# Feeding the output projection from psum in one inference step: last head pair, chunk rows, value tiles and conv state rearranged

## The chip, the cores and the metric

The kernel runs on one core of one Trainium2 chip. The core has five engines with an instruction queue each: TensorE (PE; its weight loads are listed apart as PEld), VectorE (DVE), ScalarE (ACT), GpSimd (POOL) and SyncE (SP, which only issues transfers). Each engine takes its instructions in the order in which they were compiled and waits at an instruction until the semaphores that it names are there. The metric is the device time in microseconds (us) of one execution, the median of several runs.

## The reference, cut to what matters

One layer of a decoder: a combined input projection, two kinds of token mixing side by side (attention heads and pooling), one output projection for both, and a gated feed-forward with a causal convolution. It runs once over a prompt of 2048 tokens behind 16 meta tokens, and once over 8 samples of one token with a paged cache of 4096 keys and values each.

```python
h = rmsnorm(xp, norm_mix_g)
q, k, v, u = project_mix(h, w_in)
o_attn = stick_breaking(q, k, v, q_pos, k_pos, sb_bias)       # 8 heads of 64
o_pool = multiscale_pool(u, 0, T, pool_w, pool_scale)
xp = xp + jnp.concatenate([o_attn, o_pool], axis=-1) @ w_out  # 1024 x 1024
h2 = rmsnorm(xp, norm_ffn_g)
f, conv_prompt = conv_ffn(h2, zero_prefix, w_up, conv_w, conv_b, w_down)   # d_ff 2816
y_prompt = rmsnorm(xp + f, norm_final_g)[:, N_META:]
...
k_past = cache_k[page_table].reshape(DB, PAST_LEN, H_A, DH)   # samples
v_past = cache_v[page_table].reshape(DB, PAST_LEN, H_A, DH)
f, conv_sample = conv_ffn(h2, state_conv, w_up, conv_w, conv_b, w_down)
```

## The kernel before, in words

Large products are taken three times: each operand is split into a rounded high part and the low rest (`split`, L162: ACT casts, L163, DVE subtracts, L164), and `mm3` (L166) adds high by high, high by low and low by high (L169 to L171). The text calls the products by the psum tile that they fill: pso (output projection), psu (up-projection), psd (down-projection).

**Attention.** Four head pairs are worked through, the last with hp = 3, in blocks of 128 queries (bi); a block runs over chunks of 512 keys from the last to the first. `top` marks a block's first chunk and `low` its last. `weigh` (L531) transposes the weights (tt) and multiplies them with the values into the psum tile po. At `low` a copy of po (ot, on DVE) is written to the DRAM buffer cat_s, which holds the concatenated mixer output in eight chunks of 128 rows: four of the head pairs, four of the pooling. `finished` collects the blocks of the last pair.

**Output projection.** `out_tile` (L619) takes a finished block: it reads all eight chunks back from cat_s (cr, L623), splits them into ch and cl, and fills two pso halves of 24 products each, so 48. DVE adds the residual rows (xt, L633); the sum goes to xp_s (L634), its norm is taken (`rstd_of`: one pass of ACT and some ten small instructions of DVE), and the normed tile goes to h_s (L638; h2_s in the code). The out tiles are called in the loop over the attention's units, one behind.

**Up-projection.** The normed rows are needed transposed, in four chunks of 512 tokens. `h2_first` (L731) makes chunks 0 and 1: eight loads of 512 KB (xn, L737) from the ring "uwr", which also takes the weights, and eight transposes for each (L741). `h2_chunk` (L753) makes chunk 2 at the fifth of 44 passes (it == 4) and chunk 3 at the 22nd: two loads of 1 MB each (L759) in the ring "kvd" of four slots, and 32 transposes (L766) through a single psum bank ("tp3"). Between the two the conv states of the samples are read and transposed (sc, L773 and L776). Each pass does two half passes, one for each of two chunks, with two psu tiles of 24 products.

**Decode.** Beside the up-projection the samples' attention runs, by a list `order`: key tiles (`decode_keys`, two DVE instructions each, L818 and L820), value tiles (`decode_values`, four products on PE, L886), softmax steps and a sum. `gather` (L801) fetches each 1 MB tile by an indirect transfer on POOL's queue into the kvd ring, `ahead` = 2 tiles ahead. DSTEP says how far the list has to be at each half pass.

**Down-projection.** Psd tiles, and between them the few rows of the samples and their neighbours: `few_down` (L1024, psum tile fewd) and `few_up` (L1053, tile few), fed by raw weight tiles (`load_raw`, three buffers). FSTEP says how far their list has to be.

The order of instructions on each engine is set when the kernel is compiled: a scheduler with a model of the engines (`schedule_with_timeline_sim`) arranges what the code writes, and pools hand out their slots from a free list.

Of the kernel before, what the change touches and what calls it, by code (L numbers as in the profile page):

```python
# [44 lines left out]
RAWB = 3  # L45
FSTEP = lambda i: 9 * i // 4
DSTEP = lambda i: 133 * i // 85
# [12 lines left out]
def hymba_kernel(  # L60
# [378 lines left out]
    def attention(hp):  # L439
# [162 lines left out]
    finished, wo, out_pool = [], [], {}  # L602
# [16 lines left out]
    def out_tile(bi):  # L619
        pc, gffn = out_pool["pc"], out_pool["g"]  # L620
        c0, n = TILES[bi + 1]
        cr = pc.tile([P, NK, P], F32, name="cr")
        nc.sync.dma_start(out=cr, in_=cat_s[:, :, c0:c0 + n].rearrange("c p n -> p c n"))  # L623
        ch = pc.tile([P, NK, P], F32R, name="ch", bufs=CHB)
        cl = pc.tile([P, NK, P], F32R, name="cl", bufs=CHB)
        split(ch, cl, cr)
        xt = pc.tile([P, D], F32, name="xt2", bufs=2)
        x_rows(xt, bi + 1)
        for hf in range(2):
            cs = slice(hf * 512, (hf + 1) * 512)  # L630
            ps = psm.tile([P, CW], F32, name="pso", tag="psm")
            mm3(ps, [(ch[:, c, :], cl[:, c, :], wo[c][0][:, cs], wo[c][1][:, cs]) for c in range(NK)])
            nc.vector.tensor_tensor(out=xt[:, cs], in0=ps, in1=xt[:, cs], op=ALU.add)  # L633
# [31 lines left out]
    for ui, (h, un) in enumerate(units):  # L665
# [11 lines left out]
        if ui + 1 >= END:  # L677
            if at_ < len(fill):
                fill_to(at_ + 2)
            elif len(finished) > 1:  # L680
                out_tile(finished.pop(0))
    for h_, ab, un_ in pend:
        h_[3](ab, *un_)
    for bi in finished:
        out_tile(bi)
# [42 lines left out]
    with ExitStack() as es:  # L728
        phb = es.enter_context(tc.tile_pool(name="h2b", bufs=2, reuse_waits="tile"))

        def h2_first(ch):  # L731

            h2c[ch] = (phb if ch else pha).tile([P, 2, NK, CW], F32R, name="h2c")
            for a in range(4):
                i = 1 + 4 * ch + a
                xn = puw.tile([P, NK, P], F32, name="xn0", tag="uwr").rearrange("p c n -> p (c n)")
# [32 lines left out]
        sc_v = state_conv.rearrange("b j f -> (b j) f")  # L769
        for f0 in range(0, 44, 11):  # L770
            room = dp.tile([P, 4, 512], F32, name="sc", tag="kvd").rearrange("p k f -> p (k f)")
            sc = room[:2 * NS, 0:11 * P]
            nc.sync.dma_start(out=sc, in_=sc_v[:, f0 * P:(f0 + 11) * P])  # L773
            ts = pst.tile([P, 4, P], F32, name="tp3").rearrange("p a b -> p (a b)")[:, 0:176].rearrange("p (f n) -> p f n", f=11)
            for f in range(11):
                nc.tensor.transpose(ts[:, f, :], sc[:, f * P:(f + 1) * P], ident[:2 * NS, :2 * NS])  # L776
            tv = ts.rearrange("p f (b j) -> p f b j", j=2)
            so_ = sconv[:, f0:f0 + 11, :]
            tm = room[:, 11 * P:11 * P + 11 * NS].rearrange("p (f n) -> p f n", f=11)
            bc = lambda i: par[:, 44 * i + f0:44 * i + f0 + 11].unsqueeze(2).broadcast_to([P, 11, NS])  # L780
            nc.vector.tensor_tensor(out=so_, in0=tv[:, :, :, 0], in1=bc(0), op=ALU.mult)
            nc.vector.tensor_tensor(out=tm, in0=tv[:, :, :, 1], in1=bc(1), op=ALU.mult)
            nc.vector.tensor_tensor(out=so_, in0=so_, in1=bc(3), op=ALU.add)
            nc.vector.tensor_tensor(out=so_, in0=so_, in1=tm, op=ALU.add)
# [92 lines left out]
        def decode_values(t):  # L877
            b, j = divmod(t % 64, 8)
# [3 lines left out]
            vt = kvt.pop(t)  # L882
            b4 = 32 * (b // 4)
            for k in range(4):
                kk = 31 - (4 * j + k)
                nc.tensor.matmul(ps[32 * k:32 * k + 32, :], zdec[:, b4:b4 + 32, kk], vt[:, k, :],  # L886
                                 start=j == 0, stop=j == 7, skip_group_check=True)
            if j < 7:
                return
# [28 lines left out]
        for b in range(0, NB - 2, 2):  # L918
            order += [("w", b)] + [t for x in range(16) for t in (8 * b + 16 + x, 64 + 8 * b + x)]
        order += [("w", NB - 2)] + list(range(112, 128)) + [("s", 0)]  # L920
        tiles = [t for t in order if not isinstance(t, tuple)]
        ahead = KVB - 2
# [4 lines left out]
        def decode_to(n):  # L927
            while done[0] < min(n, len(order)):
                t = order[done[0]]
                done[0] += 1  # L930
                if isinstance(t, tuple):
                    decode_weights(t[1]) if t[0] == "w" else decode_sums()
                    continue
                (decode_keys if t < 64 else decode_values)(t)
                if done[1] < 128:
                    gather(tiles[done[1]])
                    done[1] += 1

        ws_next = ws_first
        for it in range(2 * NF):  # L940
# [10 lines left out]
            if it == 4:  # L951
                h2_chunk(2)
            for k in (2 * half, 2 * half + 1):
# [32 lines left out]
    with ExitStack() as es:  # L986
# [12 lines left out]
        def final_norm(xt, n, dst):  # L999
            y = pd.tile([P, D], F32, name="y", bufs=3)  # L1000
# [39 lines left out]
        def few_norm():  # L1040
            few_add()
            gf = pd.tile([P, D], F32, name="gf", tag="y", bufs=3)
# [10 lines left out]
        def few_up(t):  # L1053
# [5 lines left out]
            for j in range(4):  # L1059
# [108 lines left out]
```

## Time and profile before

| what | value |
|---|---|
| median of 3 runs | 2836.47 us (2836.27 to 2837.02) |
| the profiled execution | 2838.09 us, span 2836.4 us |
| granted TensorE clock, mean | 0.982 |
| PE busy | 2708.9 us (96%) in 14623 instructions |
| DVE, ACT, POOL busy | 1806.2, 1039.8 and 816.5 us |
| transfers | 500.87 MB, mean 177 GB/s |

The profile follows one execution. Its stages on the time axis: input projection and attention to about 985 us, the last head pair with the output projection to 1153, the passage to the up-projection to 1203, the up-projection with the decode to about 2270, the down-projection to the end. A row of a timeline gives the start, the duration, the engine, the line and operation, the tile written and the tile read, and in brackets the idle time of the engine before it and what ended it. A row of waits gives who waited for whom, the total, how often, and the longest.

### The profile page before, as it was taken

The numbers are of one execution on the slowest core, as the hardware profiler recorded it, in microseconds if no ns is written. First come the engines' busy times: TensorE is split into PE (matmuls) and PEld (weight loads), VectorE is DVE, ScalarE is ACT, GpSimd is POOL, SyncE is SP. The second block draws the span as 40 slices with busy tenths as digits, with TensorE's granted clock in tenths as the row PEclk, the third lists the DMA queues.
The fourth block names the chain that finished last, engine by engine and source line by source line (L and its number), as shares of the span: only waits on it lengthen the run. The fifth ranks groups of instructions, "written<-read, shape, count | busy, mean of one in ns | idle before, by whom it ended". The sixth has DMA issues, their size and how long they took to land.

```text
span 2836.4 us, 39537 instructions
## 1 busy us (share of the span) xinstructions
PE 2708.9 (96%) x14623; PEld 2093.9 (74%) x14623; DVE 1806.2 (64%) x2989; ACT 1039.8 (37%) x1801; POOL 816.5 (29%) x995
## 2 busy tenths in 40 slices
PE   5899999999999999699999998999999999999998
PEld 4677777777776877588777776777777767777766
DVE  4588668867578678589867765877673441124433
ACT  4466557655565355322222222322222220012111
POOL 0132233332233122054545453545443200000000
PEclk9999999999999999799999999999999999999999
DMA  7642542455435432566675655556556385556562
GB/s 257 224 166 100 174 166 93 139 197 165 145 105 181 137 100 93 155 215 211 214 243 194 210 201 189 197 175 226 201 171 223 112 282 187 181 184 202 164 208 77
DMA packets 325287, 500.87 MB, mean 177 GB/s; under 512 B 24280, under 2 KB 233448, under 8 KB 308694
## 3 DMA queue, kind: packets, MB, share of 16 engines
q1 hardware_dynamic: 306661, 364.12, 39.6%
q0 software_dynamic: 18432, 134.23, 12.8%
q8 instruction: 115, 1.88, 0.3%
q14 instruction: 79, 0.64, 0.1%
HBM read 397.04 MB, written 101.64 MB: 176 GB/s over the span
## 4 chain that ended last, share of the span: by engine, by line
PE 76%; DVE 11%; DMA 5%; issue 4%; ACT 2%; POOL 1%; SPq 0%; DVEq 0%; POOLq 0%; ACTq 0%
PE psu L169 10%; PE psu L170 10%; PE psu L171 10%; PE psd L169 5%; PE psd L171 5%; PE psd L170 5%; PE po L567 4%; PE psm L169 4%; PE psm L170 4%; PE psm L171 3%; DVE om L517 3%; PE z L509 3%; PE tt L552 3%; PE dav L886 2%; PE pso L169 1%
## 5 line engine op out<-in xcount | busy, mean ns | idle before, releaser
L169 PE MATMUL psu<-h2c,uwh 128*128 128x512 f32 x1408 | 554.2, 394 | 0.7 <-ACT h2c L163 0.7
L170 PE MATMUL psu<-h2c,uwh 128*128 128x512 f32 x1408 | 551.6, 392 | 0.0
L171 PE MATMUL psu<-h2c,uwl 128*128 128x512 f32 x1408 | 551.2, 392 | 0.0
L517 DVE TENSOR_TENSOR_SCAN om<-om,zero 128x513 f32<-128x513 f32 (+5 forms) x360 | 379.1, 1061 | 86.2 <-ACT om L510 48.9
L522 POOL TENSOR_TENSOR be<-be,om 128x512 f32<-128x512 f32 (+3 forms) x176 | 188.1, 1069 | 554.7 <-DVE om L517 354.7
L966 DVE SCALAR_TENSOR_TENSOR cv<-psu,par,cv 128x511 f32<-128x511 f32 x352 | 260.8, 742 | 129.4 <-ACT cv L963 128.4
L169 PEld LDWEIGHTS psu<-h2c,uwh 128*128 128x128 f32 x1408 | 265.2, 188 | 79.7 <-issue 14.1
L170 PEld LDWEIGHTS psu<-h2c,uwh 128*128 128x128 f32 x1408 | 265.1, 188 | 64.5 <-issue 10.7
L171 PEld LDWEIGHTS psu<-h2c,uwl 128*128 128x128 f32 x1408 | 265.0, 188 | 63.8 <-issue 9.0
L977 POOL TENSOR_TENSOR cv<-cv,cv 128x512 f32<-128x512 f32 x88 | 198.1, 2251 | 267.8 <-DVE cv L971 217.5
L510 ACT ACTIVATE om<-z,nbias 128x512 f32<-128x512 f32 (+5 forms) x360 | 213.2, 594 | 164.7 <-PE z L509 95.4
L1135 DVE TENSOR_TENSOR xt<-psd,xt 128x512 f32<-128x512 f32 x64 | 44.1, 690 | 293.7 <-PE psd L171 293.6
L963 ACT ACTIVATE cv<-psu,par 128x512 f32<-128x512 f32 x176 | 136.5, 776 | 249.2 <-PE psu L171 238.4
L164 DVE TENSOR_TENSOR uwl<-uwr,uwh 128x1024 fp32r<-128x1024 f32 x94 | 127.3, 1356 | 148.4 <-ACT uwh L163 146.0
L511 ACT ACTIVATE be<-z,bias 128x512 f32<-128x512 f32 (+5 forms) x360 | 211.8, 592 | 2.3 <-DVE bm L527 1.2
L170 PE MATMUL psm<-hk,wh 128*128 128x512 f32 x512 | 207.3, 405 | 3.3 <-DVE hk L218 3.2
L169 PE MATMUL psm<-hk,wh 128*128 128x512 f32 x512 | 205.8, 407 | 3.6 <-ACT hk L217 3.2
L171 PE MATMUL psm<-hk,wl 128*128 128x512 f32 x512 | 205.0, 401 | 1.1 <-DVE wl L164 1.1
L171 PE MATMUL psd<-wd,al 128*128 128x512 f32 x512 | 201.1, 393 | 0.0
L169 PE MATMUL psd<-wd,ah 128*128 128x512 f32 x512 | 200.8, 396 | 0.0
L170 PE MATMUL psd<-wd,ah 128*128 128x512 f32 x512 | 200.6, 392 | 0.0
L163 ACT CAST uwh<-uwr 128x1024 fp32r<-128x1024 f32 x94 | 98.9, 1055 | 267.5 <-PE psu L170 254.9
(236 smaller groups left out, 4831.5 us busy)
## 6 DMA issues: line engine op xcount, KB each, us to landing
hk<-hs_s SPq DMA_DIRECT2D x96, 512.0 KB
uwr<-in_w_up_dram SPq DMA_DIRECT2D x88, 512.0 KB
act_s<-sg SPq DMA_DIRECT2D x88, 256.0 KB
ar<-act_s SPq DMA_DIRECT2D x32, 704.0 KB
raw<-in_w_up_dram SPq DMA_DIRECT2D x40, 512.0 KB
xt<-in_x_prompt_dram SPq DMA_DIRECT2D x32, 512.0 KB
hs_s<-hk SPq DMA_DIRECT2D x32, 512.0 KB
uwr<-in_w_down_dram SPq DMA_DIRECT2D x22, 512.0 KB
```

The lines of the kernel that those rows point to most:

```text
L164: nc.vector.tensor_tensor(out=lo, in0=src, in1=f32(hi), op=ALU.subtract)
L169: nc.tensor.matmul(ps, ah, bh, start=i == 0, stop=False)
L170: nc.tensor.matmul(ps, ah, bl, start=False, stop=False)
L171: nc.tensor.matmul(ps, al, bh, start=False, stop=i == n - 1)
L510: nc.scalar.activation(out=om[:M, e, 0:n], in_=z[:M, :n], func=AF.Sigmoid, scale=-SCALE, bias=nbias[:M, h:h + 1])
L511: nc.scalar.activation(out=be[:M, e, 0:n], in_=z[:M, :n], func=AF.Sigmoid, scale=SCALE, bias=bias[:M, h:h + 1])
L517: nc.vector.tensor_tensor_scan(out=rv, data0=rv, data1=zero[:M, 0:1].broadcast_to([M, n + 1]), initial=1.0 if top else st["prev"][:M, e, 0 ...
L522: (nc.gpsimd if cnt["mul"] % 2 == 0 else nc.vector).tensor_tensor(out=be[:M, e, m0:n], in0=be[:M, e, m0:n], in1=om[:M, e, m0 + 1:n + 1], o ...
L567: mm = nc.tensor.matmul(o, v_, a_, start=top and i < (2 if groups else 1), stop=low and i == len(prods) - 1, skip_group_check=True)
L963: nc.scalar.activation(out=t, in_=ps, func=AF.Identity, scale=cpar(2, fi), bias=cpar(3, fi))
L966: nc.vector.scalar_tensor_tensor(out=t[:, o:], in0=ps[:, 0:CW - o], scalar=cpar(d, fi), in1=t[:, o:], op0=ALU.mult, op1=ALU.add)
L977: nc.gpsimd.tensor_tensor(out=cv[1], in0=cv[0], in1=cv[1], op=ALU.mult)
```

## The change

It has five parts.

1. The last pair's blocks (hp == 3) no longer pass through cat_s. `out_rows` is called when a block begins, reads seven of the eight chunks in two transfers, splits them and loads the residual rows. When the last product of po is done, po itself is split into the eighth chunk of ch and cl, and `out_tile` follows at once. The chunk of the last pair comes last in the products (list KO).
2. The loads of `h2_first` take their buffers from three rings in turn, and `h2_chunk` transposes into the six psum banks of psu.
3. The samples' conv states are made at the 13th pass.
4. Value tiles are worked two at a time, the gathers run three tiles ahead, and the list has fewer steps (DSTEP).
5. In the down-projection there are four raw buffers, `few_up` takes two tiles at a time, and FSTEP is less steep; the result tile y has two buffers, not three.

```diff
-RAWB = 3
-FSTEP = lambda i: 9 * i // 4
-DSTEP = lambda i: 133 * i // 85
+RAWB = 4
+FSTEP = lambda i: 3 * i // 2
+DSTEP = lambda i: 101 * i // 85
...
             if top:
                 st["po"] = psd.tile([P, P], F32, name="po")
+                if hp == 3 and bi >= 0:
+                    st["out"] = out_rows(bi)
...
             if low:
+                if hp == 3 and bi >= 0:
+                    split(st["out"][0][:, NK - 1, :], st["out"][1][:, NK - 1, :], po)
+                    out_tile(bi, *st["out"])
+                    return
                 ot = pb.tile([P, P], F32, name="ot")
                 nc.vector.tensor_copy(ot[:, :M], po[:, :M])
                 nc.sync.dma_start(out=cat_s[hp, :, NS + q0:NS + q0 + M], in_=ot[:, :M])
-                if hp == 3 and bi >= 0:
-                    finished.append(bi)
...
+    KO = [0, 1, 2, 4, 5, 6, 7, 3]
...
+    def out_rows(bi):
+
+        pc = out_pool["pc"]
+        c0, n = TILES[bi + 1]
+        cr = pc.tile([P, NK - 1, P], F32, name="cr")
+        for a, b in ((0, 3), (4, NK)):
+            nc.sync.dma_start(out=cr[:, a - a // 4:b - a // 4, :], in_=cat_s[a:b, :, c0:c0 + n].rearrange("c p n -> p c n"))
+        ch = pc.tile([P, NK, P], F32R, name="ch", bufs=CHB)
+        cl = pc.tile([P, NK, P], F32R, name="cl", bufs=CHB)
+        split(ch[:, 0:NK - 1, :], cl[:, 0:NK - 1, :], cr)
+        xt = pc.tile([P, D], F32, name="xt2", bufs=2)
+        x_rows(xt, bi + 1)
+        return ch, cl, xt
...
-            mm3(ps, [(ch[:, c, :], cl[:, c, :], wo[c][0][:, cs], wo[c][1][:, cs]) for c in range(NK)])
+            mm3(ps, [(ch[:, i, :], cl[:, i, :], wo[c][0][:, cs], wo[c][1][:, cs]) for i, c in enumerate(KO)])
...
-                xn = puw.tile([P, NK, P], F32, name="xn0", tag="uwr").rearrange("p c n -> p (c n)")
+                xn = puw.tile([P, NK, P], F32, name="xn0", tag=("uwr", "uwh", "uwl")[(a + ch) % 3]).rearrange("p c n -> p (c n)")
...
-                        tp = pst.tile([P, 4, P], F32, name="tp3")
+                        tp = psm.tile([P, 4, P], F32, name="tp3c", tag="psu")
...
-        sc_v = state_conv.rearrange("b j f -> (b j) f")
...
+        def sample_conv():
+            sc_v = state_conv.rearrange("b j f -> (b j) f")
...
         def decode_values(t):
...
-            vt = kvt.pop(t)
...
+            for e in range(2):
+                vt = kvt.pop(t + e)
+                for k in range(4):
+                    kk = 31 - (4 * (j + e) + k)
+                    nc.tensor.matmul(ps[32 * k:32 * k + 32, :], zdec[:, b4:b4 + 32, kk], vt[:, k, :],
+                                     start=j + e == 0, stop=j + e == 7, skip_group_check=True)
...
-        ahead = KVB - 2
+        ahead = KVB - 1
...
             if it == 4:
                 h2_chunk(2)
+            if it == 12:
+                sample_conv()
...
-            y = pd.tile([P, D], F32, name="y", bufs=3)
+            y = pd.tile([P, D], F32, name="y", bufs=2)
...
-            for j in range(4):
-                nc.tensor.matmul(few[0][32 * j:32 * j + 32, 0:w], hsm[:, c, :], raw[t][:, w * j:w * (j + 1)],
-                                 start=c == 0, stop=c == NK - 1, skip_group_check=True)
+            for e in range(2):
+                for j in range(4):
+                    nc.tensor.matmul(few[0][32 * j:32 * j + 32, 0:w], hsm[:, c + e, :], raw[t + e][:, w * j:w * (j + 1)],
+                                     start=c + e == 0, stop=c + e == NK - 1, skip_group_check=True)
...
-                 [lambda t=t: few_up(t) for t in range(NK, NK + 48)] + [few_act] +
+                 [lambda t=t: few_up(t) for t in range(NK, NK + 48, 2)] + [few_act] +
...
-        uses = [2] * 4 + [0] + [1] * 48 + [0] + [2] * 11 + [0]
+        uses = [2] * 4 + [0] + [2] * 24 + [0] + [2] * 11 + [0]
```

What the scheduler makes of it is seen in the order of the engines. First PE around the last attention product of the kernel, before the change; woh and wol are the weights of the output projection, one number for each of the eight chunks (9680 is the chunk of the last pair), and L741 makes the transposes for chunks 0 and 1.

```order
L567 MATMUL po<-at,vt 64x128 x6
L567 MATMUL po<-atm,vtm 128x128
L169 MATMUL pso<-woh_9552,ch 128x512
L170 MATMUL pso<-wol_9553,ch 128x512
L169 MATMUL pso<-woh_9552,ch 128x512
L170 MATMUL pso<-wol_9553,ch 128x512
L741 MATMUL tp_12980<-ident,xn_12978 128x128 x4
L741 MATMUL tp_12988<-ident,xn_12978 128x128 x4
L171 MATMUL pso<-woh_9552,cl 128x512
```

After the last po all 48 products of the last tile follow, from its first chunk on, with eight transposes among them. The same place after the change:

```order
L569 MATMUL po<-at,vt 64x128 x6
L569 MATMUL po<-atm,vtm 128x128
L171 MATMUL pso<-woh_9745,cl 128x512
L169 MATMUL pso<-woh_9751,ch 128x512
L170 MATMUL pso<-wol_9752,ch 128x512
L171 MATMUL pso<-woh_9751,cl 128x512
L169 MATMUL pso<-woh_9805,ch 128x512
L170 MATMUL pso<-wol_9806,ch 128x512
L171 MATMUL pso<-woh_9805,cl 128x512
L169 MATMUL pso<-woh_9680,ch 128x512
L170 MATMUL pso<-wol_9681,ch 128x512
...
L748 MATMUL tp_12980<-ident,xn_12978 128x128 x4
```

Thirty-five of the 48 products have moved ahead of the last po; seven follow it, then six with the chunk of the last pair (two of the six are shown), and only then the 64 transposes. At a tile in the middle of the stage 17 instructions of PE (z, tt and pso) stand between a tile's last po and the first product of chunk 9680.

Second, SP in the passage to the up-projection, before the change, where L737 loads the rows for chunks 0 and 1 and L638 writes the normed rows of an output tile:

```order
L634 DMA xp_s<-xt_12877 128x1024
L696 DMA uwr<-in_w_up_dram 128x8x128 x2
L737 DMA xn_13057<-h_s 128x1024
L737 DMA xn_13073<-h_s 128x1024
L737 DMA xn_13089<-h_s 128x1024
L737 DMA xn_13105<-h_s 128x1024
L638 DMA h_s<-xn_12932 128x1024
L696 DMA uwr<-in_w_up_dram 128x8x128 x2
L773 DMA sc<-in_state_conv_dram 16x1408 x4
```

And after it, where L744 loads the rows and L650 writes the last tile's:

```order
L703 DMA uwr<-in_w_up_dram 128x8x128 x2
L646 DMA xp_s<-xt_12760 128x1024
L744 DMA xn_13089<-h_s 128x1024
L744 DMA xn_13057<-h_s 128x1024
L744 DMA xn_13073<-h_s 128x1024
L703 DMA uwr<-in_w_up_dram 128x8x128 x2
L650 DMA h_s<-xn_12932 128x1024
L744 DMA xn_13105<-h_s 128x1024
L703 DMA uwr<-in_w_up_dram 128x8x128
```

The weights have moved ahead of xp_s, the loads of the conv state are gone, and the last of the row loads, xn_13105, now stands behind the last write of h_s.

Third, chunk 2 on PE. Before, its groups of four transposes stand one by one among the products of the up-projection, the next group 27 to 57 rows later:

```order
L171 MATMUL psu<-h2c,uwl 128x512
L766 MATMUL tp_13891<-ident,xn_13889 128x128 x4
L169 MATMUL psu<-h2c,uwh 128x512
```

After, all of it stands in one place; tp3c are the transposes in the banks of psu:

```order
L171 MATMUL psu<-h2c,uwl 128x512
L773 MATMUL tp3c<-ident,xn_13811 128x128 x16
L773 MATMUL tp3c<-ident,xn_13841 128x128 x16
L169 MATMUL psu<-h2c,uwh 128x512
L170 MATMUL psu<-h2c,uwh 128x512
```

The 32 transposes have moved together, the two loads that feed them (xn_13811 and xn_13841) are used one right after the other, and the second load waits for the last transpose of the first, whose slot in the ring it takes.

More of the change, by code (lines that the diff above doesn't have):

```diff
@@ L617, in load_out, with out_tile @@
             nc.sync.dma_start(out=out_pool["g"], in_=norm_ffn_g.partition_broadcast(P))
-    def out_tile(bi):
+    def out_rows(bi):
[10 more added lines that the diff above has]
+        return ch, cl, xt
+    def out_tile(bi, ch, cl, xt):
         pc, gffn = out_pool["pc"], out_pool["g"]
         c0, n = TILES[bi + 1]
[L622 to L628, printed above, removed]
         for hf in range(2):
@@ L677, in hymba_kernel @@
         if ui + 1 >= END:
[L678 to L681, printed above, removed]
+            fill_to(at_ + 2)
     for h_, ab, un_ in pend:
         h_[3](ab, *un_)
-    for bi in finished:
-        out_tile(bi)
     main.close()
@@ L767, in h2_chunk @@
                         split(h2c[ch][:, 0, c4:c4 + 4, a * P:(a + 1) * P], h2c[ch][:, 1, c4:c4 + 4, a * P:(a + 1) * P], tp)
-        sc_v = state_conv.rearrange("b j f -> (b j) f")
[L770 to L784, printed above, removed]
@@ new lines, in sample_conv @@
+        def sample_conv():
+            sc_v = state_conv.rearrange("b j f -> (b j) f")
+            for f0 in range(0, 44, 11):
+                room = dp.tile([P, 4, 512], F32, name="sc", tag="kvd").rearrange("p k f -> p (k f)")
+                sc = room[:2 * NS, 0:11 * P]
+                nc.sync.dma_start(out=sc, in_=sc_v[:, f0 * P:(f0 + 11) * P])
+                ts = pst.tile([P, 4, P], F32, name="tp3").rearrange("p a b -> p (a b)")[:, 0:176].rearrange("p (f n) -> p f n", f=11)
+                for f in range(11):
+                    nc.tensor.transpose(ts[:, f, :], sc[:, f * P:(f + 1) * P], ident[:2 * NS, :2 * NS])
+                tv = ts.rearrange("p f (b j) -> p f b j", j=2)
+                so_ = sconv[:, f0:f0 + 11, :]
+                tm = room[:, 11 * P:11 * P + 11 * NS].rearrange("p (f n) -> p f n", f=11)
+                bc = lambda i: par[:, 44 * i + f0:44 * i + f0 + 11].unsqueeze(2).broadcast_to([P, 11, NS])
+                nc.vector.tensor_tensor(out=so_, in0=tv[:, :, :, 0], in1=bc(0), op=ALU.mult)
+                nc.vector.tensor_tensor(out=tm, in0=tv[:, :, :, 1], in1=bc(1), op=ALU.mult)
+                nc.vector.tensor_tensor(out=so_, in0=so_, in1=bc(3), op=ALU.add)
+                nc.vector.tensor_tensor(out=so_, in0=so_, in1=tm, op=ALU.add)
@@ L881, in decode_values @@
             ps = dav[0]
-            vt = kvt.pop(t)
             b4 = 32 * (b // 4)
[L884 to L888, printed above, removed]
+            for e in range(2):
[4 more added lines that the diff above has]
+                                     start=j + e == 0, stop=j + e == 7, skip_group_check=True)
+            if j < 6:
                 return
@@ L918, in hymba_kernel @@
         for b in range(0, NB - 2, 2):
-            order += [("w", b)] + [t for x in range(16) for t in (8 * b + 16 + x, 64 + 8 * b + x)]
-        order += [("w", NB - 2)] + list(range(112, 128)) + [("s", 0)]
-        tiles = [t for t in order if not isinstance(t, tuple)]
-        ahead = KVB - 2
+            order += [("w", b)] + [t for x in range(0, 16, 2) for t in (8 * b + 16 + x, 8 * b + 17 + x, ("v", 64 + 8 * b + x))]
+        order += [("w", NB - 2)] + [("v", t) for t in range(112, 128, 2)] + [("s", 0)]
+        tiles = []
+        for t in order:
+            tiles += [t] if not isinstance(t, tuple) else [t[1], t[1] + 1] if t[0] == "v" else []
+        ahead = KVB - 1
         done = [0, ahead]
@@ L930, in decode_to @@
                 done[0] += 1
[L931 to L937, printed above, removed]
+                kind, t = t if isinstance(t, tuple) else ("k", t)
+                {"k": decode_keys, "v": decode_values, "w": decode_weights}.get(kind, lambda t: decode_sums())(t)
+                for _ in range({"k": 1, "v": 2}.get(kind, 0)):
+                    if done[1] < 128:
+                        gather(tiles[done[1]])
+                        done[1] += 1
         ws_next = ws_first
@@ L1041, in few_norm @@
             few_add()
-            gf = pd.tile([P, D], F32, name="gf", tag="y", bufs=3)
+            gf = pd.tile([P, D], F32, name="gf", tag="y", bufs=2)
             nc.sync.dma_start(out=gf[:NSO, :], in_=norm_ffn_g.partition_broadcast(NSO))
```

4 lines of the change are left out of this document (2 added, 2 removed).

## The prediction

> **What bounds the kernel now.** I read the page's chain first, then the windows stage by stage, then the waits of TensorE (PE), and last the chain's pieces and the timeline around each long wait.
>
> ```profile
> span 2836.4 us, 39537 instructions
> ...
> PE 76%; DVE 11%; DMA 5%; issue 4%; ACT 2%; POOL 1%; SPq 0%; DVEq 0%; POOLq 0%; ACTq 0%
> ```
>
> PE carries the chain that ended last. So a microsecond is won where PE stands still or runs at half clock, and lost where the change makes it do so. The windows show the stages (start:end, length, busy time of PE, PEld, DVE, ACT, POOL with instructions, PE clock, DMA share, GB/s).
>
> ```profile
> 985.00:1153.00 168.00, 160.48 (x1041) 126.27 (x1039) 127.13 (x224) 82.92 (x158) 39.28 (x81) 0.99 0.30 97
> 1153.00:1203.00 50.00, 25.88 (x123) 21.73 (x123) 24.78 (x56) 14.18 (x23) 0.04 (x1) 0.73 0.64 187
> 1278.00:1349.00 71.00, 68.92 (x314) 56.85 (x313) 70.79 (x77) 21.12 (x30) 33.82 (x20) 1.00 0.64 214
> 1739.00:1757.00 18.00, 7.65 (x38) 3.57 (x38) 9.53 (x12) 3.71 (x6) 8.29 (x6) 0.70 0.68 232
> 2150.00:2200.00 50.00, 50.00 (x237) 36.12 (x236) 18.73 (x42) 12.35 (x16) 17.41 (x14) 1.00 0.63 227
> 2272.00:2343.00 71.00, 65.73 (x289) 47.46 (x288) 33.84 (x51) 19.94 (x21) 2.56 (x2) 0.95 0.82 278
> ```
>
> PE is full through most of the up-projection (50.00 of 50). It is idle in the last head pair (7.5 of 168), in the passage to the up-projection (24 of 50), at the load of chunk 3 (10 of 18) and at the start of the down-projection. The waits name the causes (total, times, longest).
>
> ```profile
> PE pso L169 <- ACT ch L163: 13.7, 4, 7.5
> PE tp L741 <- DMA xn<-h_s: 8.6, 3, 6.4
> PE tp L776 <- DMA sc<-in_state_conv_dram: 8.0, 1, 8.0
> PE tp L766 <- DVE h2c L164: 6.2, 4, 2.9
> PE psd L169 <- ACT ah L163: 4.1, 1, 4.1
> PE dav L886 <- DMA kvd<-in_cache_v_dram,idx: 3.8, 1, 3.8
> ```
>
> Six waits, some 44 us, and the change touches the stage of each.
>
> **Part A, out-projection tiles straight from psum.** The round trip through cat_s stands in the chain after the last attention product (start, length, what):
>
> ```profile
> 1151.86 1.23 PE po L567 x14
> 1153.43 2.02 DMA cat_s<-ot
> 1155.47 3.98 DMA cr<-cat_s
> 1159.48 1.05 ACT ch L163
> 1174.88 0.23 PE pso L171
> ```
>
> Behind the last po the last tile still waits for a write of 2.02, a read of 3.98 and a split of 1.05, and then all its 48 products follow, until 1175.11 (22.0 us after 1153.1). The clock is half for the first of them:
>
> ```profile
> 1160.57:1165.60 5.03, 5.03 (x16) 4.25 (x17) 2.53 (x5) 1.17 (x2) 0.00 (x0) 0.50 0.83 275
> ```
>
> After the change 42 of each tile's 48 products need only the seven older chunks, which are read and split when the block begins; the last six need a 128x128 split of po. Behind the last po stand 13 products instead of 48, seven of which cover that split (7 x 0.23 = 1.6 us). The products do not vanish: 35 x 0.23 = 8 us of them now fill earlier idle time. So A is worth at most the idle time: 7.5 within the stage, 7.5 behind the last po, and the half clock (2.5 of the 5.03 us, some 2 us for shorter spells and for eight transposes that move back): 20 us. At the low end the stage's own chain (DVE 127 of 168) holds on to the 7.5 us in it, and each new wait on DVE costs some more: 6 us. I take **15**: the wait behind the last po goes for certain, most of the rest goes.
>
> **Part B, passage to the up-projection.** Timeline (start, duration, engine, line, operation, idle before):
>
> ```profile
> 1157.58 0.34 SPq L638 DMA_DIRECT2D h_s<-xn  x1
> 1175.15 0.69 DVE L633 TENSOR_TENSOR xt<-pso,xt 128x512 f32<-128x512 f32 x1 [4.30 <-PE pso L171]
> 1184.16 1.94 PE L741 MATMUL tp<-ident,xn 128*128 128x128 f32 x8 [6.43 <-DMA xn<-h_s]
> 1187.15 0.60 SPq L638 DMA_DIRECT2D h_s<-xn  x1
> 1201.07 1.35 PE L776 MATMUL tp<-ident,sc 16*128 16x16 f32 x11 [8.02 <-DMA sc<-in_state_conv_dram]
> 1203.12 0.78 PE L169 MATMUL psu<-h2c,uwh 128*128 128x512 f32 x1
> ```
>
> And the load of one 512 KB row tile, from the chain:
>
> ```profile
> 1185.13 4.94 DMA xn<-h_s
> ```
>
> From the last pso (1175.1) to the first psu (1203.1) pass 28.0 us, the last 8.0 waiting for the sample's conv state, now moved away, and 6.4 for the row loads, which three rings let start earlier. What is late next: the order puts the eighth row load on SP behind the write of h_s of the last tile, which waits for its norm on DVE. In before that write comes 12.0 us after the last addition starts, with five splits between; now eight splits stand in that chain and both halves' additions come last, so 13. Then the load (4.94), eight transposes at half clock (1.94, the row above) and their split: 13 + 5 + 2 = **20, a gain of 8**. For the tile before, with DVE free, the write came 5.7 us behind its products, which ended when the po at 1151.86 began: at that price the gain is 15; if the load queues behind weights, gain 4.
>
> **Part C, chunk 2 in six banks (before the fifth pass).** Before, its eight groups of four transposes are spread between main products, with one wait:
>
> ```profile
> 1294.95 0.37 SPq L759 DMA_DIRECT2D xn<-h_s  x1
> 1302.67 0.63 PE L766 MATMUL tp<-ident,xn 128*128 128x128 f32 x4 [2.08 <-DMA xn<-h_s]
> 1174.95 2.78 PE L741 MATMUL tp<-ident,xn 128*128 128x128 f32 x24
> ```
>
> 24 transposes take 2.78 at full clock, so four take 0.46: 8 x 0.46 + 2.08 = 5.8 us. After, PE's order has 16 transposes, 16 more, and no main product between. The second 1 MB load takes the ring slot of the first, so it starts only when the first 16 transposes are done, and PE stands through it. A 1 MB load took 7.7 us from issue to use (1302.67 less 1294.95), a 512 KB one 4.94: I take 6.6 of idle time. The first load follows a decode tile on DVE that ends about when PE arrives: 0 to 7.7, taken 4.5. Transposes: 16 between full clock (2.78 for 24 gives 1.9) and half (1.94 for 8 gives 3.9): 2.9; the second 16 at half, 3.9; the split at the end 0.8. Sum 4.5 + 2.9 + 6.6 + 3.9 + 0.8 = 18.7, less 5.8: **a loss of 13** (6 to 20). It is the largest term against the change.
>
> Both waits are long enough for the clock: after 7.5 us idle it was half for 5.03 us of work (the rows of A). By the Trainium skill, "TensorE: Matmul & The Clock Gate", section "What's actually happening", one idle window of about 3.4 us halves the clock and about 3.4 us of sustained work restores it. By that rule the two restarts would lose 3.4 us and C be a loss of 13.3, by the row 5.0 and a loss of 15, since the sum above holds 3.0 for them. The trace agrees on the halving and has the longer spell.
>
> The load's price has a page too. By the Trainium skill, "DMA: Bandwidth & Descriptors", section "Anatomy of one DMA — SWDGE (gpsimd) path", a transfer takes about 2.0 us and its bytes at 436 GB/s; by that estimate 1 MB is 4.4 us, and C would be a loss of 11. The path described there is the gather's, and the trace has 7.7 for a load that shares the engines, so the row decides.
>
> **Part D, conv state at the thirteenth pass.** Four groups of 11 transposes cut into the main products, some 0.8 each (1.35 at half clock, the row in B); in before three of them did so too, and the fourth's wait is counted in B. So 3.2 less 2.4, and a new wait: the first load follows a decode tile on DVE as in C. It is bounded by nothing and 8.0 (its wait before, behind weight loads); alone it is small, so 3.5. **Loss of 4.3** (1 to 9).
>
> **Part E, chunk 3.** Before, it takes PE nearly the whole window 1739 to 1757, through one bank:
>
> ```profile
> 1750.58 1.98 PE L886 MATMUL dav<-kvd,zdec 128*32 128x512 f32 x8 [3.77 <-DMA kvd<-in_cache_v_dram,idx]
> 1756.80 1.65 PE L169 MATMUL psu<-h2c,uwh 128*128 128x512 f32 x3 [0.68 <-ACT h2c L163]
> ```
>
> 17.9 us, of which 2.2 are two value tiles. After, 32 transposes stand in one run and six banks take the splits, so the waits on DVE (6.2) go, and the value tile's wait of 3.77 goes because its gather now starts further ahead. The second load waits for a value tile just ahead of the run: 5 us. 5 + 4.5 of transposes + 0.8 = 10.3 against 15.7: **gain 5.5** (0 to 10).
>
> **Part F, value tiles in pairs.** One tile's products cost 1.1 us, three in a run 2.85:
>
> ```profile
> 2143.90 1.12 PE L886 MATMUL dav<-kvd,zdec 128*32 128x512 f32 x8
> 2139.76 2.85 PE L886 MATMUL dav<-kvd,zdec 128*32 128x512 f32 x24
> kvd<-in_cache_v_dram,idx POOLq DMA_INDIRECT x64, 7.3
> ```
>
> Pairing saves little per tile (0.1 to 0.2), and in the order 34 tiles still stand alone: 1.3. Against it, the 16 last value tiles come in 6.7 half passes instead of 10.2, so transfers rise there from the 227 GB/s of the window at 2150 to some 320 (a pair, 2.1 MB, in the 10.9 us of 48 products, beside some 120 for weights and results), where a share of 0.63 for 227 makes 360 the full rate. Two gathers of 7.3 have that spacing to land in, one behind the other, and a second pair of slots besides. I take 2 for late weights: **a loss of 0.5** (from 6 lost to 2 won).
>
> **Part G, few rows in pairs, four raw buffers.** In the down-projection:
>
> ```profile
> 2710.05 1.03 PE L1032 MATMUL fewd<-raw,asam 128*10 128x512 f32 x4
> 2718.79 1.05 PE L1032 MATMUL fewd<-raw,asam 128*10 128x512 f32 x8
> 2701.83 1.89 PE L1032 MATMUL fewd<-raw,asam 128*10 128x512 f32 x12
> ```
>
> Half a pair (x4) costs as much as a whole one (x8). In the trace 13 groups stand as x4, 5 as x12, one as x8: 24. In the new order they are five x8 and five x16; with x16 at the 1.9 of x12, 15. That is 9 saved; the groups of few become longer and fewer at the same price per tile, and I count them at nothing. Four raw loads ahead of the stage's first tile share a window at 0.82, so 2 back: **gain 7** (3 to 10).
>
> **Sum**: 15 + 8 - 13 - 4.3 + 5.5 - 0.5 + 7 = 17.7. The profiled execution took 2838.1 us (span 2836.4), 1.6 above the median of 2836.47, so it would come to 2820.4 and the median to **2819**.
>
> **The rivals.** The second of them rests on the scans of the attention, by their row among the costliest groups:
>
> ```profile
> L517 DVE TENSOR_TENSOR_SCAN om<-om,zero 128x513 f32<-128x513 f32 (+5 forms) x360 | 379.1, 1061 | 86.2 <-ACT om L510 48.9
> ```
>
> 1. *The new loads eat the gain.* C's two waits and D at their upper ends (20 and 9) and F at 6 cost 17 more: 2836, within the noise. For it speaks DVE at 70.79 of 71 around 1300, which delays the decode tile that frees the slot; against it that fewer key tiles now stand ahead (8 instead of 10).
> 2. *The split of po comes late in every tile.* It stands on DVE between scans (1.06 us each), and the two accumulators stay held meanwhile, so the next tile waits too. Sixteen tiles at x us each cost 16x; from x = 1.5 on (17.7 + 5.7, over 16) the kernel is slower. At x = 1.7 it takes 2846. For it: DVE at 127 of 168. Against: the order puts some 17 instructions of PE, about 3 us, between a tile's last po and the first product that needs it.
> 3. *The second load of chunk 2 is hidden.* Then C costs what it did before and E is at its upper end: 13 + 4.5 better, about 2801. The shared ring slot speaks against it.
> 4. *The rings do not help.* If the row loads still run behind weights and h_s as before, and the wait for sc is only replaced, B is 0, 8 less: 2827. The sc rows are gone from that place in the order, which speaks against it.
>
> **How the numbers follow.** Forecast as summed, 2808 to 2830: 0.60. Rival 1: 0.13. Rival 2: 0.08. Rival 3: 0.11. Rival 4: 0.08. A measurement of this kernel can tell about 0.2% (5.7 us): faster, below 2830.8, are the forecast and rivals 3 and 4, less 0.01 for the forecast's edge: 0.78; same 0.14; slower 0.08. Range 2801 to 2835: it leaves out rival 2 and about half of rivals 1 and 3.
>
> **What would show it.** A: no wait of pso for ch longer than 2 us, and some 5 us between the last po and the last pso. B: about 20 us from there to the first psu, with the last row load behind the write of h_s. C: a run of transposes at the fifth pass with a gap of 5 to 8 us between the sixteenth and the seventeenth and a dip of the clock. D: 11-column transposes in the thirteenth pass, with a wait for sc under 5 us. E: no wait of transposes for h2c beyond 1 us. G: ten groups of fewd. The forecast is wrong if pso waits for cl in most tiles, if PE's waits for gathers exceed 6 us, or if C's gap is missing.

## The result and the profile after

| | before | after |
|---|---|---|
| median | 2836.74 us (2836.27 to 2837.79, 4 runs) | 2814.22 us (2813.1 to 2817.6, 4 runs) |
| profiled execution, span | 2838.09 us, 2836.4 us | 2817.6 us, 2815.9 us |

The ratio is 0.9922, with a 95% interval from 0.9905 to 0.9939: 22.5 us faster. The forecast was 2819, with a range from 2801 to 2835. Between the two profiled executions the spans differ by 20.5 us, and that difference can be followed stage by stage. The table takes the start of the first product of a stage from both timelines (the end of the last pso is where the next product starts); psu products are counted 96 to a pass.

| stretch | before | after | gain |
|---|---|---|---|
| start to the end of the last pso | 1174.9 | 1162.8 | 12.1 |
| passage: last pso to first psu | 28.2 | 20.8 | 7.4 |
| passes 1 to 6 (chunk 2 is turned here) | 139.6 | 155.4 | -15.8 |
| passes 7 to 19 (conv state in the 13th) | 312.5 | 309.2 | 3.3 |
| passes 20 to 24 (chunk 3) | 137.5 | 128.9 | 8.6 |
| pass 25 to the first psd | 483.8 | 486.1 | -2.3 |
| first 132 products of psd (two blocks of 128 rows) | 43.6 | 50.2 | -6.6 |
| the rest, to the last psd | 506.6 | 492.8 | 13.8 |

Three of these rows do not compare the same work, since value tiles have moved between them. Counted by their products in the traces, eight to a tile, passes 7 to 19 work 16 of the 64 tiles instead of 20, passes 20 to 24 work 10 instead of 8, and the passes behind work 38 instead of 36. At 1.1 us a tile the first of these stretches is relieved of 4.4 us and each of the others takes on 2.2. So the 3.3 is no gain, the -2.3 is no loss, and for the same work the gain at chunk 3 is nearer 11 than 8.6.

The windows of the changed kernel, in the columns of the prediction: the last head pair without idle time, the passage, and the start of the down-projection.

```profile
970.00:1140.00 170.00, 170.00 (x1103) 135.69 (x1104) 139.38 (x256) 94.13 (x183) 41.56 (x85) 1.00 0.30 100
1163.00:1183.00 20.00, 9.30 (x61) 8.47 (x60) 16.67 (x37) 10.25 (x18) 0.00 (x0) 0.77 0.89 296
2263.00:2313.00 50.00, 42.99 (x185) 29.28 (x185) 26.67 (x41) 16.57 (x17) 2.57 (x2) 0.90 0.83 289
```

The waits of PE (total, times, longest) that answer to those of before:

```profile
PE tp3c L773 <- DMA xn<-h_s: 16.0, 3, 9.7
PE tp L748 <- DVE rt L153: 5.8, 1, 5.8
PE tp L748 <- DMA xn<-h_s: 3.7, 1, 3.7
PE psd L169 <- ACT ah L163: 3.6, 1, 3.6
PE psd L170 <- DVE wd L164: 3.0, 1, 3.0
PE tp3c L773 <- DVE h2c L164: 2.1, 1, 2.1
PE pso L169 <- DVE xt L645: 1.8, 1, 1.8
```

No wait of pso for ch is left, and none for sc. The largest wait is new: tp3c for row loads, 14.6 of the 16.0 us at chunk 2. In the timeline of PE and SP that place reads:

```profile
1275.45 0.37 SPq L766 DMA_DIRECT2D xn<-h_s  x1
1282.41 3.64 PE L773 MATMUL tp3c<-ident,xn 128*128 128x128 f32 x16 [9.69 <-DMA xn<-h_s]
1286.09 0.36 SPq L766 DMA_DIRECT2D xn<-h_s  x1
1290.98 3.65 PE L773 MATMUL tp3c<-ident,xn 128*128 128x128 f32 x16 [4.93 <-DMA xn<-h_s]
```

The load was issued 2.7 us after PE had arrived (1282.41 less 9.69 is 1272.72) and took 7.0; the second was issued when the first run was done and took 4.9. Both runs of 16 transposes went at half clock, 3.64 and 3.65 us. The two waits and the two runs make 21.9 us. The granted clock is the third figure from the end, 0.50 in both:

```profile
1282.40:1286.00 3.60, 3.59 (x16) 3.25 (x16) 1.85 (x2) 1.76 (x3) 1.36 (x2) 0.50 0.26 94
1291.00:1294.60 3.60, 3.60 (x17) 3.60 (x18) 1.55 (x3) 1.76 (x3) 0.00 (x0) 0.50 0.48 196
```

### The profile page after: what moved, and what is told of

It reads as the page before. It is cut to its first block, busy times and chain, and to the rows that moved or that the text cites. A ratio compares the mean times of both kernels' runs of the same rounds, so it can differ in the third digit from the quotient of the medians.

```text
span 2815.9 us, 39585 instructions
## 1 busy us (share of the span) xinstructions
PE 2699.1 (96%) x14623; PEld 2102.5 (75%) x14623; DVE 1800.5 (64%) x2989; ACT 1041.7 (37%) x1817; POOL 837.1 (30%) x995
## 4 chain that ended last, share of the span: by engine, by line
PE 84%; DVE 6%; DMA 4%; issue 3%; ACT 2%; POOL 1%; SPq 0%; POOLq 0%; DVEq 0%; ACTq 0%
PE psu L169 11%; PE psu L170 11%; PE psu L171 11%; PE psd L169 6%; PE psd L171 6%; PE psd L170 6%; PE po L569 5%; PE psm L169 4%; PE psm L170 4%; PE z L509 4%; PE psm L171 4%; PE tt L554 3%; DVE om L517 2%; PE dav L896 2%; PE pso L171 2%
## 5 line engine op out<-in xcount | busy, mean ns | idle before, releaser
L990 POOL TENSOR_TENSOR cv<-cv,cv 128x512 f32<-128x512 f32 x88 | 226.3, 2572 | 386.3 <-DVE cv L984 306.9
L164 DVE TENSOR_TENSOR uwl<-uwr,uwh 128x1024 fp32r<-128x1024 f32 x94 | 121.3, 1293 | 125.2 <-ACT uwh L163 122.8
```

The source lines that it names most:

```text
L164: nc.vector.tensor_tensor(out=lo, in0=src, in1=f32(hi), op=ALU.subtract)
L990: nc.gpsimd.tensor_tensor(out=cv[1], in0=cv[0], in1=cv[1], op=ALU.mult)
```

## The experiments

In e1 to e6 and e9 one part of the changed kernel is put back, e7 is the kernel before with one part, e8 and e10 to e12 build on what was found. Ratios are to the kernel before.

**e1: chunk 2 through one bank.**

```diff
-                        tp = psm.tile([P, 4, P], F32, name="tp3c", tag="psu")
+                        tp = psm.tile([P, 4, P], F32, name="tp3c", tag="psu") if ch == 3 else pst.tile([P, 4, P], F32, name="tp3")
```

> The changed kernel with chunk 2 turned through the one old bank again; chunk 3 keeps the six banks. In the changed kernel PE stands 9.7 and 4.9 us before the two runs of 16 transposes of chunk 2 and works them at half clock (3.65 us each), some 22 us in all. Theory (six banks let the compiler's order put all 32 transposes in one place, where PE has to wait for both loads): with one bank the order spreads them over about 250 products again, the waits go, chunk 2 costs some 6 us, the median falls by 15 to about 2799. Rival (the rows come late whatever the bank): the waits move into the spread groups, and the time stays between 2808 and 2814.

Measured: 2794.45 us, ratio 0.9846 (0.9829 to 0.9862), 20 us under the changed kernel. The transposes stand apart again and wait for nothing. The first and the last of the eight groups, from PE's timeline of e1:

```profile
1283.38 0.60 PE L773 MATMUL tp<-ident,xn 128*128 128x128 f32 x4
...
1341.73 0.60 PE L773 MATMUL tp<-ident,xn 128*128 128x128 f32 x4
```

Passes 1 to 6 take 134.6 us, not 155.4. The first load was issued 7.8 us before its first group (1275.61), so it may have been no quicker than the 7.0 of the changed kernel; with products of psu between, PE does not wait for it. The second load was issued at 1284.59, before the first one's groups were through, and so no longer stands behind their last transpose. The rival is out.

The edit changes two things at once: how many banks there are, and that they are those of psu, whose next tiles then take their turn behind the transposes. Which of the two draws the run together was not tested.

**e9: chunk 3 through one bank as well.** The edit of e1 without its condition.

> As e1, with chunk 3 through the one old bank too; all else as in the changed kernel. Against e1 (2794) it shows what the six banks are worth at chunk 3. Theory (there the rows are loaded in time and the waits were for the splits of one bank, 6.2 us in the kernel before): 4 to 10 us slower than e1, 2799 to 2804. Rival (the gain at chunk 3 came from the value tiles' earlier gathers): within 3 us of e1.

Measured: 2806.16 us, ratio 0.9889 (0.9874 to 0.9904), 11.7 us over e1, a little more than the theory's range. Passes 20 to 24 take 140.9 us here, 130.8 in e1. PE's timeline of e9 at chunk 3:

```profile
1716.22 1.97 PE L896 MATMUL dav<-kvd,zdec 128*32 128x512 f32 x8 [4.91 <-DMA kvd<-in_cache_v_dram,idx]
1718.12 1.12 PE L773 MATMUL tp<-ident,xn 128*128 128x128 f32 x4
1720.64 1.11 PE L773 MATMUL tp<-ident,xn 128*128 128x128 f32 x4 [1.40 <-DVE h2c L164]
1723.15 1.12 PE L773 MATMUL tp<-ident,xn 128*128 128x128 f32 x4 [1.40 <-DVE h2c L164]
1725.67 1.11 PE L773 MATMUL tp<-ident,xn 128*128 128x128 f32 x4 [1.40 <-DVE h2c L164]
```

And of the changed kernel there:

```profile
1722.76 1.94 PE L773 MATMUL tp3c<-ident,xn 128*128 128x128 f32 x16 [1.36 <-DMA xn<-h_s]
1726.84 3.56 PE L773 MATMUL tp3c<-ident,xn 128*128 128x128 f32 x16 [2.15 <-DVE h2c L164]
```

The wait for a value tile (4.91) comes back although the gathers still run three ahead and in pairs; so it belongs to the order around the transposes, not to the decode list. (e4, below, shows the other side: six banks, two gathers ahead, and no wait for a value tile.) Six banks win at chunk 3, where chunk 0's place must be free first and the products that follow need the result, and lose at chunk 2, where nothing needs it for 17 passes.

**e2: the last pair's result through DRAM again.** `finished`, `out_tile` and the copy ot as before; all else stays.

> The changed kernel with the last head pair's result written to DRAM and read back as before. Theory (the round trip costs PE idle time in the last head pair, 7.5 us behind the last product and 7.5 within the stage, and half clock): the waits of pso for ch come back, 12 us by the two traces, so about 2826. Rival (the stage's own chain on DVE sets its length, and the gain seen there came from the row loads and the conv state moved out of the way): within 4 us of the changed kernel, 2814 to 2818.

Measured: 2822.01 us, ratio 0.9948 (0.9932 to 0.9965), 7.8 us over the changed kernel: between theory and rival. The waits are back (window 960 to 1200 of e2):

```profile
PE pso L169 <- ACT ch L163: 13.6, 5, 7.5
```

The last pso ends 12.7 us later, as the theory said, but the passage takes 13.0 us instead of 20.8. In e2 five of the eight row loads were issued and the first two weight tiles split before the last pso ended; in the changed kernel four loads and no weight tile, so more of that work lies bare. That this cover is what shortens the passage is argued from the two orders, not tested alone. So a gain of 12 in one stage is worth 5 at the first psu.

**e7: the first part alone, in the kernel before.** `out_rows`, KO and the split of po; all else as before.

> The kernel before with the first part of the change alone: the last pair's result split from psum, out_tile at once. Theory (it shortens the stage by 12 us whatever follows, and the passage stays at its 28, bounded by row loads and sc): 2823 to 2827. Rival (as e2 against the changed kernel suggests, what the stage wins is partly lost in the passage, because the norm of the last tile now comes closer to it): 2828 to 2833.

Measured: 2824.85 us, ratio 0.9953 (0.9936 to 0.9969): 11.9 us faster. The last pso ends 11.4 us earlier, the passage takes 30.4 (28.2 before), so 9.2 are left at the first psu. The theory's time is met; its passage was a little too short.

**e5: one ring for the row loads.**

```diff
-tag=("uwr", "uwh", "uwl")[(a + ch) % 3]
+tag="uwr"
```

> The changed kernel with the loads of the eight row tiles in the ring uwr alone again. In the changed kernel 21.0 us pass from the last pso to the first psu, in e2 13.3; in e2 and here the order has the last row load ahead of the last write of h_s, in the changed kernel behind it. Theory (that place, behind DVE's norm of the last tile, sets the passage): it takes 13 to 16 us here, the time is 2806 to 2810. Rival (three rings are what lets the loads start early): with one ring they wait for one another's transposes and for weights, the passage takes 20 to 25, the time is 2814 to 2818.

Measured: 2817.0 us, ratio 0.9928 (0.9912 to 0.9945), not told apart from the changed kernel; the passage takes 21.3 us. Both lines of thought fail: the last row load stands ahead of the last write of h_s here and nothing is won, and with one ring instead of three next to nothing is lost.

**e6: the conv state ahead of the up-projection.** `sample_conv()` is called before the decode is set up, not at it == 12.

> The changed kernel with the samples' conv state read and turned ahead of the up-projection, as before. Theory (moving it won a wait of PE at the end of the passage and cost little later): the passage takes 3 to 9 us longer, since the four sc loads stand behind the last row load; three groups of transposes move with it and weigh the same: 2817 to 2822. Rival (the wait for sc hides behind the last row load, which is late anyway, and the later place costs the 4.3 us of the forecast): 2809 to 2813.

Measured: 2818.81 us, ratio 0.9933 (0.9916 to 0.9949), 4.6 us over the changed kernel. The passage takes 27.6, of which PE's timeline of e6 shows

```profile
1187.41 1.35 PE L784 MATMUL tp<-ident,sc 16*128 16x16 f32 x11 [4.88 <-DMA sc<-in_state_conv_dram]
```

and passes 1 to 6 take 3.0 more for the other groups, while passes 11 to 14 take 4.8 less. In the changed kernel the groups wait for nothing there:

```profile
1492.88 0.85 PE L784 MATMUL tp<-ident,sc 16*128 16x16 f32 x11
1499.67 0.85 PE L784 MATMUL tp<-ident,sc 16*128 16x16 f32 x11
1505.44 0.85 PE L784 MATMUL tp<-ident,sc 16*128 16x16 f32 x11
```

So the move is worth 6.8 in the passage and costs 1.8 later.

**e3: the few rows' tiles one at a time.** RAWB, FSTEP, `few_up`, `uses` and the buffers of y as before.

> The changed kernel with the few rows' tiles one at a time, three raw buffers and the old steps. Theory (a lone half pair of the product fewd costs as much as a whole one): the groups of fewd are again mostly half pairs, about 9 us more of PE time late in the down-projection; the waits at its start (3.6 and 3.0 us in the changed kernel) get smaller by about 3, so about 2821. Rival (the saving comes back as waits for raw loads): 2812 to 2816.

Measured: 2822.98 us, ratio 0.9946 (0.9929 to 0.9963), 8.8 us over the changed kernel. In PE's timelines of the late down-projection e3 has, among its groups,

```profile
2697.43 1.03 PE L1045 MATMUL fewd<-raw,asam 128*10 128x512 f32 x4
2706.16 1.05 PE L1045 MATMUL fewd<-raw,asam 128*10 128x512 f32 x8
```

and the changed kernel

```profile
2694.56 1.05 PE L1045 MATMUL fewd<-raw,asam 128*10 128x512 f32 x8
2710.91 1.90 PE L1045 MATMUL fewd<-raw,asam 128*10 128x512 f32 x16
```

Four or eight products cost the same, as the forecast said, and the changed kernel has ten groups of fewd, five x8 and five x16, as forecast. The first 132 products of psd take 43.9 us in e3 and 50.2 in the changed kernel, the rest 506.0 and 492.8: more is won late, and more lost at the start, than forecast.

**e4: value tiles one at a time, two gathers ahead.** `decode_values`, the list and DSTEP as before.

> The changed kernel with the decode list of before: value tiles one at a time, two gathers ahead. Theory (pairs save little on PE, and the denser last gathers cost about as much): 2810 to 2816, and chunk 3 keeps a wait of some 4 us for a value tile near it. Rival (pairs and the third gather ahead are what shortens chunk 3): chunk 3 costs 6 us more again, 2820.

Measured: 2810.78 us, ratio 0.9907 (0.9890 to 0.9923), 3.4 us under the changed kernel, with overlapping intervals. Of that, 3.0 stand in the profiled executions at the first psu, where no value tile has run yet. Up to there such differences reach 5 us between executions of one and the same order (first psu at 1178.7 in e9, 1184.0 in e1). So the pairs are within a few microseconds of nothing, on which side stays open. By stages there is more to see: passes 7 to 19 take 314.3 us in e4 and 309.2 in the changed kernel, where four fewer value tiles stand in them, and passes 20 to 24 take 124.3 and 128.9, of which two more value tiles are 2.2 and waits about the rest (PE idles 0.9 us there in e4, 3.5 in the changed kernel). The wait of some 4 us for a value tile, which the theory kept, did not come; the rival is out.

**e8: e1 and e4 together.**

> e1 and e4 together: chunk 2 through one bank, value tiles one at a time with two gathers ahead; the rest of the change stays. If the two effects add (20 and 3.4 us below the changed kernel): 2790 to 2793. If pairs lose only because of the waits in chunk 2: 2794 to 2797.

Measured: 2793.15 us, ratio 0.9843 (0.9827 to 0.9860), 1.3 under e1. The first time was expected if the effects add, the second if they do not; 2793.15 lies between the two ranges, and the difference from e1 is within the noise, so the run does not decide it.

**e10: weights after all row tiles.** In e8,

```diff
         h2_first(0)
-        ws_first = [load_up(0), load_up(NF)]
         h2_first(1)
+        ws_first = [load_up(0), load_up(NF)]
```

> e8 with the first two weight tiles of the up-projection asked for after all eight row tiles, not between the two chunks. In the changed kernel the row loads come in three lots (at 1153 to 1160, 1168 and 1176 us), since six of the nine ring slots go to weights; e5 shows that the number of rings and the place behind the write of h_s do not matter by themselves. Theory (the slots set the passage): all rows are loaded in one lot, the passage from the last pso to the first psu falls from 21 to 12 to 16, the time to 2784 to 2789. Rival (then the weights come late, and their splits end the passage instead): 19 to 23, 2792 to 2796.

Measured: 2792.51 us, ratio 0.9840 (0.9826 to 0.9853); passage 19.9 us. All eight row loads were issued ahead of the last pso's end, and the theory of the slots still falls; passage and time are the rival's. SP and PE in the timeline of e10:

```profile
1149.69 8.76 SPq L744 DMA_DIRECT2D xn<-h_s  x8
1160.08 0.38 SPq L703 DMA_DIRECT2D uwr<-in_w_up_dram  x1
1162.80 5.18 PE L748 MATMUL tp<-ident,xn 128*128 128x128 f32 x32 [1.01 <-PE tp L748]
1177.29 1.97 PE L748 MATMUL tp<-ident,xn 128*128 128x128 f32 x8 [9.30 <-DVE h2c L164]
```

PE now waits 9.30 for a psum bank that DVE has not emptied.

**e11: one weight tile between the chunks, one behind.** The edit of e10 with `load_up(0)` left in its place.

> e8 with the first weight tile between the chunks and the second after both. Under the theory of the slots the rows come in two lots: passage 16 to 19, 2788 to 2791; under its rival (DVE's work, the same in all these kernels, sets it) 20 to 22, 2792 to 2796.

Measured: 2793.0 us, ratio 0.9847 (0.9834 to 0.9861); passage 20.7 us. These are the rival's numbers, but not its cause: what PE waits for there is a row load, and for DVE only 0.8 us.

```profile
PE tp L748 <- DMA xn<-h_s: 7.7, 2, 7.0
PE tp L748 <- DVE h2c L164: 0.8, 1, 0.8
```

**e12: e10 with DVE relieved.** The subtractions of the first two weight tiles and the clearing of zdec on GpSimd:

```diff
-        ws_first = [load_up(0), load_up(NF)]
+        ws_first = [load_up(0, nc.gpsimd), load_up(NF, nc.gpsimd)]
...
-        last_dve = nc.vector.memset(zdec, 0.0).ins
+        nc.gpsimd.memset(zdec, 0.0)
+        last_dve = last_sel
```

(`on` is passed through to `split`; last_sel is the last reduction of msel on DVE.)

> e10 with three pieces of DVE's work in the passage given to POOL, which is idle there: the low parts of the first two weight tiles (1.23 us each, with a wait of 2.46 for the second) and the clearing of zdec (1.76). In e10 all eight row loads are issued before the last pso ends and the passage still takes 19.9 us; PE waits 9.3 of it for a split on DVE that stands behind these pieces. Theory (DVE's work in its order sets the passage, once the loads come early): the last splits come 5 to 6 us sooner, the passage takes 14 to 16, the time is 2787 to 2790. Rival (the weight tiles, which now come last, end it anyway, and POOL's slower pass makes that worse): 18 to 21, 2791 to 2795.

Measured: 2795.22 us, ratio 0.9858 (0.9842 to 0.9875); passage 19.6 us. The theory falls too. DVE and ACT in the timeline of e12:

```profile
1175.51 0.69 DVE L164 TENSOR_TENSOR h2c<-tp,h2c 128x512 fp32r<-128x512 f32 x1 [4.38 <-ACT h2c L163]
```

```profile
1169.96 1.04 ACT L163 CAST uwh<-uwr 128x1024 fp32r<-128x1024 f32 x1 [2.93 <-DMA uwr<-in_w_up_dram]
1173.95 1.04 ACT L163 CAST uwh<-uwr 128x1024 fp32r<-128x1024 f32 x1 [2.94 <-DMA uwr<-in_w_up_dram]
1174.90 3.51 ACT L163 CAST h2c<-tp 128x512 fp32r<-128x512 f32 x7
```

DVE is free and waits 4.38 for ACT, whose row casts stand in its order behind the casts of two weight tiles, and these wait 2.93 and 2.94 for their loads. The loads meet full transfer engines, in e10 and in e12 alike (columns as before: the last three are PE's clock, the DMA share and GB/s):

```profile
1159.00:1177.00 18.00, 7.75 (x57) 5.89 (x55) 13.73 (x30) 10.04 (x18) 0.00 (x0) 0.88 0.99 325
```

```profile
1160.00:1178.00 18.00, 9.51 (x64) 7.10 (x62) 10.29 (x28) 10.13 (x19) 5.27 (x6) 0.83 0.97 322
```

In the changed kernel the share in its passage is 0.89. So once neither slots, nor places on SP, nor DVE are in the way, the passage still takes 20 us, with the transfer engines full and ACT's order behind the weights. Which of these two would go on holding it was not taken apart.

## Why the prediction held, step by step

The time, the sign and the list of causes were right; the terms were off on both sides and cancelled in part, and that the sum came as close as it did is partly luck: C cost more than forecast, D less, and E gave more. The single edits do not add up either: what A is worth depends on what stands behind it.

- **A, forecast 15.** The stage ends 12.1 us earlier (e2: 12.7, e7: 11.4), and no pso waits for ch; from the last po to the end of the last pso pass 3.1 us, not 5. Executions of the same order differ by 5 us at this point (e4), so 12 and 15 are not told apart. By stages A and B came to 19.5 of the 23 forecast. What the sum had wrong is what A does to the passage: it allowed 1 us for it (13 where there were 12.0), but without A the passage takes 13.0 (e2) and with it 20.8, so 8 of A's 12 are given back there.
- **B, forecast 8, found 7.4: the right number, by luck, for another reason than stated.** The conv state alone is worth 6.8 there (e6). "Three rings let the loads start earlier" was wrong (e5), and the last row load does stand behind the write of h_s in the changed kernel, but in e5 and e10 it does not and the passage is the same. So the chain that the estimate of 20 us was built on is at most one of several of about that length.
- **C, forecast a loss of 13, found 17 to 20** (passes 1 to 6: 20.8 against e1, of which 3 come back by the 24th pass; 20 by the medians). The mechanism is as forecast, with the gap between the runs and the half clock; the mis-sized term is the first wait, taken as 4.5 and measured as 9.7. The second was 4.9, taken as 6.6.
- **D, forecast a loss of 4.3, found 1.8** beside the passage. The wait for sc that was put at 3.5 did not come.
- **E, forecast 5.5, found about 10** (passes 20 to 24: 8.6 against before, with two more value tiles in them; 10.1 between e9 and e1, 12 by the medians). The value tile's wait goes with the new order, as forecast, though not because of the earlier gathers (e9, e4); the second load, put at a wait of 5, kept PE from nothing; waits of 1.36 for the first load and 2.15 for a split took its place, the latter longer than the 1 us that the forecast named as a sign.
- **F, forecast a loss of 0.5**: within the noise of that (e4, e8). PE never waits for a gather in the up-projection of the changed kernel, nor for weights, so the fuller transfers that the forecast feared held nothing up. The full rate that the forecast worked with, 360 GB/s, was high at least for the passage: at a share of 0.99 it was 325 (e10).
- **G, forecast 7, found 7.2 in the trace and 8.8 in e3.** Its parts were further off: 6.6 lost at the start (forecast 2), 13.8 won later (forecast 9). The late gain is not the 9 of fewd. Counting in both timelines from each product's start to the next, less idle time, fewd takes 10.4 us there instead of 17.0, the psd products 460.5 instead of 464.0 and few 21.0 instead of 22.9, and 1.2 us of idle time are gone. At the start 2.9 of the 6.6 lost are more idle time, 2.2 are slower psd products, and 1.7 are work of the few rows that moved there; why psd got 3.5 us shorter late was not tested.

Of the rivals, none came about as a whole. The second, a late split of po, is excluded by the trace: the one wait of pso for DVE of any length that is left, 1.8 us, is for xt.

The best versions are e1, e8, e10, e11 and e12, which are not told apart: 2792.5 to 2795.2 us, about 1.5% below the kernel before and 0.7% below the changed one. What they share is the change as it is, with chunk 2 through its one bank.

## What to carry to other kernels

More psum banks, shared with the main products, let the scheduler pack work together. Here that paid where the result is needed next (chunk 3, 10 us), and cost where the work was only filler between products (chunk 2, 20 us): a run has to wait for its loads, filler does not. A stretch can also get shorter because work has moved out of it, as the value tiles did here, so count the work in each stretch before calling it a gain. A stall that is removed may have covered the work of the next stage, so price the two together, as e2 and e7 do. Where three experiments each free one suspect and the time stays, look for several chains of one length before moving the next piece.

## What the runs showed of the hardware

The clock fell to half behind a wait of only 2.15 us. The windows of the two runs of 16 transposes of chunk 3 in the changed kernel (the clock is the third figure from the end) show it: the first run, behind a wait of 1.36, went at full clock, the second at half, though no single wait there was longer than 2.15 and the two together make 3.5.

```profile
1722.70:1724.70 2.00, 1.94 (x16) 1.73 (x16) 1.20 (x4) 1.28 (x3) 0.00 (x0) 1.00 0.92 317
1726.80:1730.40 3.60, 3.56 (x17) 3.59 (x18) 3.60 (x5) 1.76 (x3) 3.52 (x2) 0.53 0.93 336
```

The length of the wait alone does not decide it: behind one of 2.11 us, which ended at 857.56 in the same trace, the granted clock was 1.00 for the next 2 us. At half clock 16 transposes cost 1.7 us more (3.64 and 1.94), on top of the wait. GpSimd took 2.34 us for a 128x1024 subtraction in e12 that DVE does in 1.23 (the same line in e2):

```profile
1171.09 2.34 POOL L164 TENSOR_TENSOR uwl<-uwr,uwh 128x1024 fp32r<-128x1024 f32 x1 [23.20 <-ACT uwh L163]
```
